# Attention scores of a pair as two 64-row halves of the array, with three products each

## The chip, the cores and the metric

The kernel runs on one core of one Trainium2 chip. Its engines are TensorE (PE in the profile; its weight loads are listed apart, as PEld), VectorE (DVE), ScalarE (ACT), GpSimd (POOL) and SyncE (SP), whose queue issues most of the transfers. The metric is the device time of one execution in microseconds.

## The reference, cut to what matters

Two layers of an encoder for 512 positions and width 1024. Each layer normalizes, projects with one matrix of 4096 columns, runs two groups of attention, gates both, and projects back. All is in float32.

```python
# per layer; q_a, k_a, v_a: 8 heads of 64; q_b, k_b: 4 heads of two maps of 64; v_b: 4 heads of 128
proj = rmsnorm(x, norm_g[l]) @ w_in[l]
# group A: every position sees an 8 x 16 window of the 8 x 64 grid
logits = einsum('bhcd,bhicjd->bhcij', qr, kr) * 64**-0.5 + bias
out_a  = softmax(logits) @ v                      # per head
# group B: two softmax maps over all 512 positions, subtracted
logits = einsum('bqhtd,bkhtd->bhtqk', qblk, k) * 64**-0.5   # t = 0, 1
p      = softmax(logits + t5_bias)
out_b  = rmsnorm((p[:, :, 0] - lam * p[:, :, 1]) @ v, subln_g) * (1 - lam_init)
x = x + concat([out_a * silu(g_a), out_b * silu(g_b)]) @ w_out[l]
```

## The kernel before, in words

Every float32 factor is held as a sum of a high and a low part in a shorter format (fp32r), and a product is computed as three: high by high, high by low, low by high. For the projections (`proj_fm`, L252, with 512 columns; `proj_tm`, L267, with 256) these are 24 matrix products per PSUM tile, 8 slices of the contraction in three terms.

A layer goes through the list `ORDER`: V units (VB, VA), Q units (QB, QA: 128 columns of q and 128 of k, so two heads of group A or the two maps of one head of group B), attention steps (AB, AA) and gates. One Q unit gives the pair that one attention step works on.

*Evacuation.* `evac_q` (L271) takes the PSUM tile of q, whose rows 0 to 63 belong to the first of the pair and 64 to 127 to the second, and makes two tiles of it, one per map or head: in each, rows 0 to 63 hold the high part (ScalarE, L276) and rows 64 to 127 the low part (VectorE, L277). `evac_k` (L282) writes the high and low parts of both k into rows 0 to 63 (L290, L291), and a transfer on SP's queue (L292) copies these rows to rows 64 to 127. So a score product contracts over 128 rows, (q high, q low) by (k high, k high), and a second one over (q high, q low) by (k low, k low): two products per map.

*Group B* (`attn_b`, L303). For each of 4 tiles of 128 queries and each of 2 maps: two products of 512 columns into `st` (L316, L317), an addition of the bias with a running minimum (L319, VectorE, a custom instruction), the exponential (L322, ScalarE). Then the weights of both maps are scaled and subtracted (L326 to L329), transposed on PE (L333), split (`split`, L205 and L206) and multiplied with v into `pv` (L338).

*Group A* (`attn_a`, L363), called once per head: the bias tile `ba` is built on GpSimd (L179). For each of 4 query tiles: two products of 256 columns into `st` (L370), addition with minimum (L376), exponential (L379), scaling (L381, L382), two transposes (L385), split; at the end eight products with v (L392).

*PSUM.* Eight banks: `ps_p` has three tiles (`pp`, projections), `ps_s` two of one bank (`st`, scores, also the first warm-up products, L462, the transposed gain, L468, and the bias table, L151), `ps_t` two (`pt`), `ps_v` one (`pv`).

*Order.* Up to the first unit the order is pinned as written (`pinned`, `held`). Behind that a planner (the Tile framework with its timeline) decides the order on each engine: it fills PE with projection products between the steps of attention. Weights come through two raw buffers (`wraw`, SP's queue, L84), are cast on ScalarE (L99), and their low part is computed on GpSimd (L101).

Of the kernel before, what the change touches and what calls it, by code (L numbers as in the profile page):

```python
# [9 lines left out]
F32 = mybir.dt.float32  # L10
F32R = mybir.dt.float32r
AF = mybir.ActivationFunctionType
# [4 lines left out]
P = 128  # L17
S = 512
# [26 lines left out]
def hybrid_encoder(ctx: ExitStack, tc: tile.TileContext, x, norm_g, w_in, na_rpb,  # L45
# [14 lines left out]
    ps_s = ctx.enter_context(tc.tile_pool(name="ps_s", bufs=2, space=PSUM))  # L60
# [15 lines left out]
    # ---------------------------------------------------------------- weights  # L76
# [47 lines left out]
    # ------------------------------------------------------- position biases  # L124
# [60 lines left out]
    # ------------------------------------------------------------- lambdas  # L185
# [22 lines left out]
    # ---------------------------------------------------------------- norm  # L208
# [35 lines left out]
    # --------------------------------------------------------- projections  # L244
# [26 lines left out]
    def evac_q(pp):  # L271
        res = []
        for m in range(2):
            q = qk.tile([P, S], F32R, name="qs", bufs=QK_BUFS)
            src = pp[64 * m:64 * m + 64, :]
            A.activation(out=q[0:64], in_=src, func=AF.Copy, scale=-0.125)  # L276
            V.scalar_tensor_tensor(out=q[64:128], in0=src, scalar=-0.125, in1=q[0:64].bitcast(F32),  # L277
                                   op0=ALU.mult, op1=ALU.subtract)
            res.append(q)
        return res  # L280

    def evac_k(pp, natural):  # L282
        kt = qk.tile([P, 4, S], F32R, name="kt", bufs=2)
        for m in range(2):
            src = pp[64 * m:64 * m + 64, :]
            kh, kl = kt[0:64, m, :], kt[0:64, 2 + m, :]
            if natural:
                src = src.rearrange("p (b r c) -> p b r c", r=ROWS, c=C8)
                kh, kl = (z.rearrange("p (r b c) -> p b r c", r=ROWS, c=C8) for z in (kh, kl))
            A.copy(out=kh, in_=src)  # L290
            V.tensor_tensor(out=kl, in0=src, in1=kh.bitcast(F32), op=ALU.subtract)  # L291
        nc.sync.dma_start(out=kt[64:128].bitcast(F32), in_=kt[0:64].bitcast(F32))  # L292
        return [(kt[:, m, :], kt[:, 2 + m, :]) for m in range(2)]
# [368 lines left out]
```

## Time and profile before

| | us |
|---|---|
| median of 3 runs | 632.57 |
| lowest and highest | 631.94, 633.4 |
| span of the profiled execution | 630.6 |
| PE busy | 591.7 |
| VectorE busy | 422.3 |
| ScalarE busy | 324.6 |
| GpSimd busy | 277.3 |

The profile gives no time of its own for the profiled execution beyond the span, which runs from the first to the last instruction. Busy time of PE is modelled at the ends of products, and neighbouring products overlap in it: a product of 512 columns lasts about 0.39 us from start to end, but the next one starts 0.23 us after it. Where it matters, starts are compared with starts.

### The profile page before, as it was taken

How to read it: one execution, taken by the hardware profiler on the slowest of the kernel's cores; microseconds unless marked ns; L12 is line 12 of the kernel's file. 1: busy time of each engine (PE TensorE's matmuls, PEld its weight loads, DVE VectorE, ACT ScalarE, POOL GpSimd, SP SyncE). 2: the span in 40 equal slices, each digit the busy share in tenths (PEclk: the TensorE clock that was granted, in tenths of full speed). 3: DMA queues.
4: the chain of work that ended last, by engine and by line, in shares of the span. 5: the costliest groups of instructions: out<-in, count | busy, mean ns of one | idle time of the engine just before them, and what ended most of it. 6: DMA issues, size and time to landing. Idle time of an engine off the chain costs nothing.

```text
span 630.6 us, 10037 instructions
## 1 busy us (share of the span) xinstructions
PE 591.7 (94%) x3626; PEld 522.3 (83%) x3626; DVE 422.3 (67%) x907; ACT 324.6 (51%) x706; POOL 277.3 (44%) x232
## 2 busy tenths in 40 slices
PE   4799699999899999999999999999989999999992
PEld 3678597888799878889999898888879878889992
DVE  3552354997988868874564257798888968874542
ACT  3343353864766555744343455666567646654421
POOL 2341422444456747743143633344535665733111
PEclk9799899999999999999999999999999999999997
DMA  6566746552442454264454452342343444355204
GB/s 145 129 124 192 213 147 197 134 136 78 109 119 55 143 129 133 85 171 146 134 168 135 123 144 86 90 114 63 88 107 93 116 116 116 101 167 168 68 1 134
DMA packets 77448, 77.57 MB, mean 123 GB/s; under 512 B 9906, under 2 KB 71346, under 8 KB 76374
## 3 DMA queue, kind: packets, MB, share of 16 engines
q1 hardware_dynamic: 75926, 74.53, 41.7%
q0 software_dynamic: 1472, 2.40, 2.3%
q8 instruction: 29, 0.48, 0.3%
q14 instruction: 21, 0.17, 0.1%
HBM read 63.16 MB, written 9.37 MB: 115 GB/s over the span
## 4 chain that ended last, share of the span: by engine, by line
PE 58%; DMA 14%; DVE 10%; issue 5%; POOL 5%; SPq 5%; ACT 3%; POOLq 0%; ACTq 0%; DVEq 0%
PE pp L252 25%; PE pp L267 22%; DMA wraw<-in_w_in_dram 4%; DMA y<-in_x_dram 4%; SPq L135 3%; DVE ea L382 2%; POOL wl L101 2%; DMA yb_d<-tb_d 2%; POOL ba L179 2%; PE pv L338 2%; DVE kt L291 2%; DVE w4k L329 1%; PE pt L333 1%; PE st L316 1%; DMA rs_d<-rsb 1%
## 5 line engine op out<-in xcount | busy, mean ns | idle before, releaser
L101 POOL TENSOR_TENSOR wl<-wraw,wh 128x1024 fp32r<-128x1024 f32 x68 | 166.2, 2462 | 192.5 <-ACT wh L99 124.9
L99 ACT CAST wh<-wraw 128x1024 fp32r<-128x1024 f32 x78 | 78.8, 1046 | 72.2 <-DMA wraw<-in_w_in_dram 28.9
L252 PE MATMUL pp<-hTh,wh 128*128 128x512 f32 x384 | 103.4, 397 | 3.2 <-DVE kt L291 3.2
L252 PE MATMUL pp<-hTh,wl 128*128 128x512 f32 x384 | 106.3, 398 | 0.0
L252 PE MATMUL pp<-hTl,wh 128*128 128x512 f32 x384 | 104.5, 398 | 0.0
L252 PEld LDWEIGHTS pp<-hTh,wh 128*128 128x128 f32 x384 | 70.4, 188 | 17.7 <-issue 3.6
L252 PEld LDWEIGHTS pp<-hTh,wl 128*128 128x128 f32 x384 | 70.3, 189 | 14.5 <-issue 0.5
L252 PEld LDWEIGHTS pp<-hTl,wh 128*128 128x128 f32 x384 | 70.2, 188 | 13.9
L267 PE MATMUL pp<-wh,hTh 128*128 128x256 f32 x256 | 72.3, 302 | 7.7 <-ACT hTh L205 4.5
L267 PE MATMUL pp<-wh,yTh 128*128 128x256 f32 x256 | 72.4, 283 | 0.0
L267 PE MATMUL pp<-wl,yTh 128*128 128x256 f32 x256 | 72.3, 283 | 0.0
L267 PE MATMUL pp<-wh,yTl 128*128 128x256 f32 x256 | 71.9, 283 | 0.0
L267 PE MATMUL pp<-wh,hTl 128*128 128x256 f32 x256 | 70.3, 293 | 0.0
L206 DVE TENSOR_TENSOR ptl<-pt,pth 128x256 fp32r<-128x256 f32 (+1 forms) x96 | 48.2, 507 | 31.6 <-ACT pth L205 30.7
L267 PE MATMUL pp<-wl,hTh 128*128 128x256 f32 x256 | 68.9, 287 | 0.0
L205 ACT CAST pth<-pt 128x256 fp32r<-128x256 f32 (+1 forms) x96 | 42.0, 443 | 43.1 <-PE pt L333 29.3
L382 DVE TENSOR_SCALAR ea<-ea,rza 128x256 f32<-128x256 f32 x64 | 58.5, 914 | 1.8
L267 PEld LDWEIGHTS pp<-wh,hTh 128*128 128x128 f32 x256 | 49.3, 202 | 10.9 <-ACT hTh L205 5.0
L179 POOL TENSOR_TENSOR ba<-nmask,ya 128x256 f32<-128x256 f32 (+1 forms) x64 | 39.6, 650 | 32.3 <-DVE mna L376 18.5
L319 DVE CUSTOM_DVE_ANT_0 lt<-st,yb 128x512 f32<-128x512 f32 x64 | 43.5, 685 | 11.2 <-PE st L317 10.7
L267 PEld LDWEIGHTS pp<-wh,hTl 128*128 128x128 f32 x256 | 48.8, 199 | 0.8
L267 PEld LDWEIGHTS pp<-wh,yTh 128*128 128x128 f32 x256 | 49.1, 192 | 0.2
(111 smaller groups left out, 1141.0 us busy)
## 6 DMA issues: line engine op xcount, KB each, us to landing
wraw<-in_w_in_dram SPq DMA_DIRECT2D x32, 512.0 KB
wraw<-in_w_in_dram SPq DMA_DIRECT2D x64, 256.0 KB
kt<-kt SPq DMA_DIRECT2D x16, 512.0 KB
wraw<-in_w_out_dram SPq DMA_DIRECT2D x16, 512.0 KB
y<-in_x_dram SPq DMA_DIRECT2D x16, 256.0 KB
ya_d<-rp_d SPq DMA_DIRECT2D x32, 120.0 KB
ya<-ya_d SPq DMA_DIRECT2D x16, 240.0 KB
yb<-yb_d SPq DMA_DIRECT2D x8, 280.0 KB
```

The source lines that it names most:

```text
L99: A.copy(out=wh[:, ks, :], in_=r)
L101: eng.tensor_tensor(out=wl[:, ks, :], in0=r, in1=wh[:, ks, :].bitcast(F32), op=ALU.subtract)
L135: eng.dma_start(out=dst[:, i * C8:(i + 1) * C8, :], in_=bass.AP(tensor=src.tensor, offset=src.offset + base - step * r - C8 * b, ap=[[pitc ...
L179: G.tensor_tensor(out=ba[:, i0:i0 + n], in0=_view(nmask, i0 * C8, [[C8, n], [0, ROWS], [1, C8]]), in1=_view(y, w0, [[C8, n], [RPW, ROWS], ...
L205: A.copy(out=oh, in_=ps)
L206: V.tensor_tensor(out=ol, in0=ps, in1=oh.bitcast(F32), op=ALU.subtract)
L252: T.matmul(out=pp, lhsT=a[:, kc, cs], rhs=b[:, kc, c0:c0 + S], start=(n == 0), stop=(n == 3 * KC - 1))
L267: T.matmul(out=pp[:, 0:256], lhsT=a[kc][:, c0:c0 + P], rhs=b[:, kc, :], start=(n == 0), stop=(n == 3 * KC - 1))
L291: V.tensor_tensor(out=kl, in0=src, in1=kh.bitcast(F32), op=ALU.subtract)
L319: V.tensor_tensor_reduce(out=lt, in0=st, in1=yb[:, 48 - 16 * qt:560 - 16 * qt], scale=1.0, scalar=3e38, op0=ALU.add, op1=ALU.min, accum_ou ...
L338: T.matmul(out=pv[:, qp * 256:(qp + 1) * 256], lhsT=vt[:, kt, h % 2, vs, :], rhs=pp[:, kt, :], start=(n == 0), stop=(n == 11))
L382: V.tensor_scalar_mul(e, e, rz)
```

## The change

The pair is computed together. `evac_q` and `evac_k` no longer rearrange rows: they evacuate all 128 rows at once, the high part with one ScalarE instruction and the low part with one VectorE instruction, and the copy of k on SP's queue is gone. A new function `scores` computes the scores of both maps or heads of the pair for one query tile into one `st` tile of two banks: the first map from rows 0 to 63, the second from rows 64 to 127. Each contracts over 64 rows, so three products are needed per map: q high by k high, q low by k high, q high by k low. The two maps alternate. `attn_a` now handles two heads, with two bias tiles at once. `ps_s` has one buffer of two banks where it had two of one, and warm-up, gain and table products use `ps_p`. `qs` keeps two buffers, which held the two maps of one unit and now hold two whole units; `kt` has two buffers of half the size; `ba` has four instead of two. The instructions behind the scores stay the same in number.

```diff
-    ps_s = ctx.enter_context(tc.tile_pool(name="ps_s", bufs=2, space=PSUM))
+    ps_s = ctx.enter_context(tc.tile_pool(name="ps_s", bufs=1, space=PSUM))
...
-            tp = ps_s.tile([P, S], F32, name="st")
+            tp = ps_p.tile([P, S], F32, name="pp")
...
-        ba = work.tile([P, 12, ROWS, C8], F32, name="ba")
+        ba = work.tile([P, 12, ROWS, C8], F32, name="ba", bufs=4)
...
     def evac_q(pp):
-        res = []
-        for m in range(2):
-            q = qk.tile([P, S], F32R, name="qs", bufs=QK_BUFS)
-            src = pp[64 * m:64 * m + 64, :]
-            A.activation(out=q[0:64], in_=src, func=AF.Copy, scale=-0.125)
-            V.scalar_tensor_tensor(out=q[64:128], in0=src, scalar=-0.125, in1=q[0:64].bitcast(F32),
-                                   op0=ALU.mult, op1=ALU.subtract)
-            res.append(q)
-        return res
+        q = qk.tile([P, 2, S], F32R, name="qs", bufs=QK_BUFS)
+        A.activation(out=q[:, 0, :], in_=pp, func=AF.Copy, scale=-0.125)
+        V.scalar_tensor_tensor(out=q[:, 1, :], in0=pp, scalar=-0.125, in1=q[:, 0, :].bitcast(F32),
+                               op0=ALU.mult, op1=ALU.subtract)
+        return q
...
-        nc.sync.dma_start(out=kt[64:128].bitcast(F32), in_=kt[0:64].bitcast(F32))
-        return [(kt[:, m, :], kt[:, 2 + m, :]) for m in range(2)]
+        A.copy(out=kh, in_=src)
+        V.tensor_tensor(out=kl, in0=src, in1=kh.bitcast(F32), op=ALU.subtract)
+        return kt
+
+    def scores(q, qs, keys):
+        st = ps_s.tile([P, 2, S], F32, name="st")
+        for n, (a, b) in enumerate(((0, 0), (1, 0), (0, 1))):
+            for m in range(2):
+                rhs = keys(b, slice(64 * m, 64 * m + 64))
+                out = st[:, m, :] if rhs.shape[-1] == S else st[:, m, 0:256]
+                T.matmul(out=out, lhsT=q[64 * m:64 * m + 64, a, qs], rhs=rhs, start=(n == 0), stop=(n == 2))
+        return st
...
+                st = scores(q, slice(qt * P, (qt + 1) * P), lambda i, ps: k[ps, i, :])
                 for m in range(2):
-                    st = ps_s.tile([P, S], F32, name="st")
-                    kh, kl = k[m]
-                    T.matmul(out=st, lhsT=q[m][:, qt * P:(qt + 1) * P], rhs=kh, start=True, stop=False)
-                    T.matmul(out=st, lhsT=q[m][:, qt * P:(qt + 1) * P], rhs=kl, start=False, stop=True)
```

The planner arranges the new program anew. The first place is PE at the first scores of the first layer, where the second projection of the pair ends and a V unit begins (L316 and L317 before, L294 after are score products; L252 and L267 are projections). Before:

```order
L252 MATMUL pp<-hTh,wl 128x512 x8
L267 MATMUL pp<-wh,hTh 128x256
L267 MATMUL pp<-wl,hTh 128x256
L316 MATMUL st<-kt,qs 128x512
L317 MATMUL st<-kt,qs 128x512
L316 MATMUL st<-kt,qs 128x512
L317 MATMUL st<-kt,qs 128x512
L267 MATMUL pp<-wh,hTl 128x256
```

And after:

```order
L252 MATMUL pp<-hTh,wl 128x512 x6
L294 MATMUL st<-kt,qs 128x512 x6
L252 MATMUL pp<-hTh,wl 128x512 x2
L252 MATMUL pp<-hTh,wh 128x512 x8
L252 MATMUL pp<-hTl,wh 128x512 x8
L252 MATMUL pp<-hTh,wl 128x512 x8
L294 MATMUL st<-kt,qs 128x512 x6
L267 MATMUL pp<-wh,hTh 128x256
```

The first group of scores moves ahead of the next unit's projection, and a whole projection stands between it and the second group.

The second place is PE in group A of the first layer (L370 before and L294 after are score products; L385 and L382 transposes; L390 products with v). Before:

```order
L370 MATMUL st<-kt,qs 128x256 x2
L252 MATMUL pp<-hTh,wh 128x512 x4
L252 MATMUL pp<-hTl,wh 128x512 x8
L252 MATMUL pp<-hTh,wl 128x512 x4
L370 MATMUL st<-kt,qs 128x256 x2
L252 MATMUL pp<-hTh,wl 128x512
L385 MATMUL pt<-ident,ea 128x128 x2
```

And after:

```order
L390 MATMUL pv<-pth,v 128x256
L390 MATMUL pv<-ptl,v 128x256
L294 MATMUL st<-kt,qs 128x256 x5
L382 MATMUL pt<-ident,ea 128x128 x2
L294 MATMUL st<-kt,qs 128x256
L382 MATMUL pt<-ident,ea 128x128 x2
```

Groups of two products each become groups of six, some of which are cut by transposes or products with v; over the program L294 stands in 88 stretches, 36 with 512 columns and 52 with 256, for 64 groups.

## Rows read from the trace of the kernel before

**Rows 1.** Page, part 1: busy us (share of the span) and instructions.
```profile
span 630.6 us, 10037 instructions
...
PE 591.7 (94%) x3626; PEld 522.3 (83%) x3626; DVE 422.3 (67%) x907; ACT 324.6 (51%) x706; POOL 277.3 (44%) x232
```

**Rows 2.** Busy us by stage (length; PE, PEld, DVE, ACT, POOL; PE clock; DMA).
```profile
39.00:175.00 136.00, 125.81 (x694) 107.23 (x693) 88.28 (x195) 69.59 (x140) 50.15 (x38) 0.97 0.55 150
175.00:283.00 108.00, 107.28 (x619) 92.49 (x617) 85.70 (x205) 64.85 (x153) 68.83 (x62) 1.00 0.44 118
283.00:573.00 290.00, 286.68 (x1794) 255.09 (x1793) 205.77 (x444) 157.26 (x344) 132.22 (x96) 1.00 0.41 117
sum 534.00, PE 519.77 PEld 454.81 DVE 379.75 ACT 291.70 POOL 251.20; mean PE 173.26 PEld 151.60 DVE 126.58 ACT 97.23 POOL 83.73
```

**Rows 3.** Chain of waits in order of time: start us, us, what.
```profile
283.40 44.42 PE pp L267 x369
327.82 0.87 PE pt L234 x8
...
347.39 18.82 PE pp L252 x81
...
366.33 0.24 PE st L316
```

**Rows 4.** Groups by line: xcount | busy us, mean ns of one | idle before, releasers.
```profile
L319 DVE CUSTOM_DVE_ANT_0 lt<-st,yb 128x512 f32<-128x512 f32 x64 | 43.5, 685 | 11.2 <-PE st L317 10.7
...
L316 PE MATMUL st<-kt,qs 128*128 128x512 f32 x64 | 26.6, 416 | 2.7 <-DMA kt<-kt 1.6 <-DVE mn L319 1.0
...
L370 PE MATMUL st<-kt,qs 128*128 128x256 f32 x128 | 25.9, 289 | 2.2 <-DMA kt<-kt 1.6 <-DVE mna L376 0.6
...
L277 DVE SCALAR_TENSOR_TENSOR qs<-pp,qs 64x512 fp32r<-64x512 f32 x32 | 22.1, 689 | 4.7 <-ACT qs L276 3.9
L291 DVE TENSOR_TENSOR kt<-pp,kt 64x512 fp32r<-64x512 f32 x32 | 21.9, 686 | 27.9 <-ACT kt L290 27.5
```

**Rows 5.** Weight loads where the table product L151 begins: start us, us, what.
```profile
32.17 0.14 PEld L234 LDWEIGHTS pt<-ident,w4k 128*128 128x128 f32 x1
32.48 0.09 PEld L151 LDWEIGHTS st<-oh,t5s 32*4 32x4 f32 x2 [0.17 <-issue]
```

**Rows 6.** Loads and products where L151 ends, from several overlapping windows.
```profile
34.28 0.19 PEld L267 LDWEIGHTS pp<-wh,hTh 128*128 128x128 f32 x1 [0.86 <-ACT wh L99]
33.34 1.02 PE L151 MATMUL st<-oh,t5s 32*4 32x512 f32 x2
34.28 0.39 PE L267 MATMUL pp<-wh,hTh 128*128 128x256 f32 x1
...
33.77 0.59 PE L151 MATMUL st<-oh,t5s 32*4 32x512 f32 x1
...
34.51 0.64 PE L267 MATMUL pp<-wh,hTh 128*128 128x256 f32 x4
```

**Rows 7.** ScalarE and VectorE in the same stretch.
```profile
31.92 1.25 ACT L205 CAST hTh<-pt 128x512 fp32r<-128x512 f32 x2 [3.54 <-PE pt L234]
...
35.36 0.42 DVE L206 TENSOR_TENSOR v<-pp,v 128x256 fp32r<-128x256 f32 x1 [1.46 <-ACT v L205]
```

**Rows 8.** Products around one with two stationary columns, L349.
```profile
121.40 0.40 PE L252 MATMUL pp<-hTh,wl 128*128 128x512 f32 x1
121.63 0.39 PE L349 MATMUL pv<-sr,ones_r 128*2 128x512 f32 x1
121.86 0.40 PE L252 MATMUL pp<-hTh,wl 128*128 128x512 f32 x1
```

**Rows 9.** Who waited for whom, PE alone: us in total, times, longest us.
```profile
PE pp L267 <- DVE kt L291: 3.2, 1, 3.2
PE pp L252 <- DVE kt L291: 3.2, 2, 1.6
```

**Rows 10.** Chain of waits near 70 us: a weight load.
```profile
67.96 4.69 DMA wraw<-in_w_in_dram
```

More of the change, by code (lines that the diff above doesn't have):

```diff
@@ L367, in attn_a @@
         for j, (k0, dk) in enumerate(A_TILES):
-            st = ps_s.tile([P, S], F32, name="st")
-            for i in range(2):
-                T.matmul(out=st[:, 0:256], lhsT=q[:, j * P:(j + 1) * P],
-                         rhs=k[i].rearrange("p (t c) -> p t c", c=P)[:, k0:k0 + dk + 1:dk, :],
-                         start=(i == 0), stop=(i == 1))
-            e = work.tile([P, 256], F32, name="ea", bufs=3)
-            mn = small.tile([P, 1], F32, name="mna")
-            i0 = (0, 4, 4, 8)[j]
@@ L383, in attn_a @@
-            pt = ps_t.tile([P, 4, P], F32, name="pt")
-            for i in range(2):
-                T.transpose(out=pt[:, i, :], in_=e[:, i * P:(i + 1) * P], identity=ident)
-            t0, sl, stp = A_SLOT[j]
-            oh, ol = (_view(p, t0 * 256 + sl * P, [[stp, 2], [1, P]]) for p in ptt)
-            split(pt[:, 0:2, :], oh, ol)
-        pv = ps_v.tile([P, S], F32, name="pv")
-        for n, (t, q0, dq) in enumerate(A_PV):
-            for i, pp in enumerate(ptt):
-                T.matmul(out=_view(pv, q0, [[dq, 2], [1, P]]), lhsT=vt[:, t, hd % 4, :],
-                         rhs=pp[:, t, :].rearrange("p (a b) -> p a b", b=P),
-                         start=(n == 0 and i == 0), stop=(n == 3 and i == 1))
@@ new lines, in attn_a @@
+            for m in range(2):
+                e = work.tile([P, 256], F32, name="ea", bufs=3)
+                mn = small.tile([P, 1], F32, name="mna")
+                i0 = (0, 4, 4, 8)[j]
+                V.tensor_tensor_reduce(out=e, in0=st[:, m, 0:256],
+                                       in1=ba[m][:, i0:i0 + 4].rearrange("p a b c -> p (a b c)"),
+                                       scale=1.0, scalar=3e38, op0=ALU.add, op1=ALU.min, accum_out=mn)
+                A.activation(out=e, in_=e, func=AF.Exp, bias=mn, scale=-1.0, accum_out=z[:, m, j:j + 1])
+                rz = small.tile([P, 1], F32, name="rza")
+                V.reciprocal(out=rz, in_=z[:, m, j:j + 1])
+                V.tensor_scalar_mul(e, e, rz)
+                pt = ps_t.tile([P, 4, P], F32, name="pt")
+                for i in range(2):
+                    T.transpose(out=pt[:, i, :], in_=e[:, i * P:(i + 1) * P], identity=ident)
+                t0, sl, stp = A_SLOT[j]
+                oh, ol = (_view(t, t0 * 256 + sl * P, [[stp, 2], [1, P]]) for t in ptt[m])
+                split(pt[:, 0:2, :], oh, ol)
@@ new lines, in attn_a @@
+        for m in range(2):
+            pv = ps_v.tile([P, S], F32, name="pv")
+            for n, (t, q0, dq) in enumerate(A_PV):
+                for i, pp in enumerate(ptt[m]):
+                    T.matmul(out=_view(pv, q0, [[dq, 2], [1, P]]), lhsT=vt[:, t, (2 * p + m) % 4, :],
+                             rhs=pp[:, t, :].rearrange("p (a b) -> p a b", b=P),
+                             start=(n == 0 and i == 0), stop=(n == 3 and i == 1))
+            tmp = work.tile([P, S], F32, name="tmpa", tag="s2", bufs=3)
+            lo = 64 * m
+            hi = 64 - lo
+            A.activation(out=tmp[lo:lo + 64], in_=pv[hi:hi + 64], func=AF.Copy, scale=0.5)
+            V.scalar_tensor_tensor(out=s_out[lo:lo + 64], in0=pv[lo:lo + 64], scalar=0.5, in1=tmp[lo:lo + 64],
+                                   op0=ALU.mult, op1=ALU.add)
@@ L459, in warm @@
     def warm(n):
-        wm = ps_s.tile([P, S], F32, name="st")
+        wm = ps_p.tile([P, S], F32, name="pp")
         for i in range(n):
@@ L465, in hybrid_encoder @@
     for i in range(2):
-        gp = ps_s.tile([P, S], F32, name="st")
+        gp = ps_p.tile([P, S], F32, name="pp")
         for j in range(4):
@@ L541, in att_a @@
             q, k = qk_t.pop(0)
[L542 to L544 removed]
+            attn_a(l, p, q, k, v.rearrange("p t h s d -> p t h (s d)"), ys[p])
         qk_t = []
```

42 lines of the change are left out of this document (12 added, 30 removed).

## The prediction, made before the changed kernel ran

> **What bounds the kernel now.** I read the busy table first, then the stages, then the chain of waits, then single matrix products. TensorE (PE) is busy 591.7 of 630.6 us, VectorE 422.3, ScalarE 324.6 [rows 1]. By stages, PE is busy 125.81 of 136 us in group B of the first layer, 107.28 of 108 in group A, and 286.68 of 290 from there to the last projection; from 39 to 573 us it is idle for 534.0 - 519.8 = 14.2 us [rows 2]. VectorE is the next one, with 85.70 of 108 us at its fullest. PE's busy time can hide gaps, because neighbouring products overlap in the trace, so I also checked the spacing on the chain of waits: 81 products of 512 columns in 18.82 us are 0.232 us each, 369 of 256 columns in 44.42 us are 0.120 us each, and a score product takes 0.24 us [rows 3]. These are long runs without a hole. So the end is set by the sum of what PE has to stream, plus some 14 us of waits, and every microsecond that a change adds to PE's own queue between 39 and 573 us shows nearly whole in the time. What it saves on VectorE, ScalarE and the DMA queues shows only where PE now waits for them.
>
> **Slots removed.** Scores now are 64 products of 512 columns at L316 and as many at L317, and 128 of 256 at L370 [rows 4]: 128 x 0.232 + 128 x 0.120 = 45.1 us of PE.
>
> **Slots added.** The new helper issues 6 products per pair instead of 4: 192 of 512 columns and 192 of 256, each with 64 rows, alternating between the upper and the lower half of the array. No product of the trace runs beside another one, so I bound this from both sides. If the two halves stream at the same time, three pairs take three slots: 96 x 0.232 + 96 x 0.120 = 33.8 us, a change of -11.3. If a half waits for the other, it is 67.6 us, a change of +22.5. Between them lies a case for which there is a near row. Each product brings its own weight load, and eight transposes, which stream little and are held up by their loads, take 0.87 us [rows 3]: one load of 128 columns every 0.109 us. If loads still follow one another and only streams overlap, a group of six has its last product start 5 x 0.109 = 0.545 us after the first, and takes 0.545 + 0.232 = 0.777 us with 512 columns (before: 0.928) and 0.665 with 256 (before: 0.480). Over 32 groups each that is 24.9 + 21.3 = 46.2 us, a change of +1.1: what group B wins, group A loses, since its short streams do not cover two loads. I take this value, since every pair of loads in the trace keeps this distance.
>
> **Changing between the two shapes.** PE enters the half-row shape and leaves it again for each stretch of score products. The order of the new program has 88 stretches of L294, not 64, because the planner cuts 24 of the groups with transposes or value products; so 176 changes. The trace has one place where the array's row split changes: the table product L151 with 32 rows amid products with 128. Going in, the last load of a transpose is at 32.17 and the next would follow 0.109 later, at 32.28; it comes at 32.48, 0.20 late, with nothing to wait for ("issue") [rows 5]. Coming out, the last two L151 products are 0.43 apart, so the slot after 33.77 ends at 34.20; the next load starts at 34.28, and its product, with the load no longer hidden behind a stream, holds the array until 34.51, that is 0.23 instead of 0.12: together 0.08 + 0.11 = 0.19 [rows 6]. The row names the cast of L99, whose output this product does not read; it reads hTh, cast by 31.92 + 1.25 = 33.17 [rows 7], so I take the delay as PE's own. At 0.19 us each, 176 changes are 33.4 us. This is the largest term, and it rests on one place with a 32-row shape; the bounds are 0 (the chip treats a half like the whole) and 0.20 (35.2 us).
>
> A counter-row stands beside it: the product with a 2-column stationary operand, L349, starts 0.23 us after its neighbour (121.40 to 121.63) and is followed after another 0.23 [rows 8]. So narrowing the columns costs nothing, and splitting the rows does. The Trainium skill, TensorEngine Tiling (Array Packing), section Key Properties, says that changing the tiling mode, and not merely the tile, drains the engine. By that rule both places should have stalled; the trace agrees for the 32-row one (0.19 to 0.20 us) and not for the 2-column one. Taken for rows alone the rule gives the 33.4 us, taken by L349's row 0.
>
> **Evacuation and copies.** Each of 16 projection units loses two of its four VectorE subtractions (0.689 and 0.686 us [rows 4]), 22.0 us in all, since 128 partitions are done at once, and two of its four ScalarE casts. Both engines are covered by PE, so in itself this is worth nothing; were PE not there, it would be worth up to those 22 us. The 16 copies of k leave SP's queue, so the weight loads behind them no longer wait for the subtractions that each copy needs, and q has room for two units instead of one. What PE can gain is its waits: 1.6 + 1.6 us for the copy [rows 4] and 3.2 + 3.2 us for L291, which releases a projection's PSUM tile [rows 9], 9.6 in all, and at the utmost all of its 14.2 us of idleness. Half of the second goes with half of the subtractions; behind the copy stands the subtraction, which stays, so of the first I count half too: -4.8, bounds 0 and -14.2.
>
> **The added wait.** ps_s had two buffers of one bank; now it has one tile of two. The next six products wait until both reductions of the previous tile are read; before, the first two waited for the first reduction only. Queued behind the waiting product on PE is everything else: projections, transposes and value products, and with them the weights' buffers. PE waits 1.0 + 0.6 us for reductions now; one reduction more is 0.685 us [rows 4]. The planner puts projection work between groups, as the order shows, so I take twice the present wait, +1.6, bounds 0 and +5. At the start, warm-up and table products move to the projections' ring of three, and the third projection of the first unit must wait for the second's value cast, which VectorE ends at 35.36 + 0.42 = 35.78, instead of starting at 34.28 [rows 6, 7]: 1.5 us. Further on PE waits behind a weight load that lands at 67.96 + 4.69 = 72.65 [rows 10], whatever PE did before, so I count 0, bound +1.5.
>
> **The sum.** -45.1 + 46.2 + 33.4 - 4.8 + 1.6 = +31.3. The profiled span is 630.6 us and the median of the runs 632.57, so 2.0 lies around the span; I leave that as it is. 630.6 + 31.3 + 2.0 = **663.9**. With the other ends of the small terms (-14.2 to 0 for the relief, 0 to 6.5 for the waits, 0.18 to 0.20 per change) the same case gives 651 to 675.
>
> **Rivals.**
> (a) The halves load and stream wholly side by side, and changes cost as in the trace: -11.3 instead of +1.1, so 651.5. For it: the halves use other rows and other banks. Against: no two loads in the trace overlap. The Trainium skill, TensorE: Matmul & The Clock Gate, section Part 3, tells of four 32-row tiles of 512 columns that ran 3.07 times as fast as in turn. By that figure, an estimate, a product of a pair takes 0.77 of a perfect overlap's rate and the scores 33.8 / 0.77 = 44 us, 2 us off my middle; no run here shows it.
> (b) The halves run in turn: 663.9 - 1.1 + 22.5 = 685.3. For it: products in the trace start strictly in turn.
> (c) **Faster**: the change of shape between 64 and 128 rows costs nothing, as with L349. Then 663.9 - 33.4 = 630.5 with loads in turn and 618.1 with loads side by side. Its place is the 176 borders, and it decides from a price per border: with side-by-side loads the kernel gets faster below (11.3 + 3.2) / 176 = 0.08 us, with loads in turn below 0.01. Against it: 0.19 in the only row that splits rows.
> (d) The diff does not do what it says: borders are free but halves run in turn: 630.5 - 1.1 + 22.5 = 651.9, the 6-for-4 products then being a plain addition.
>
> **How the numbers follow.** Forecast (borders cost, streams overlap, loads in turn) 0.45; (a) 0.17; (b) 0.10; (c) 0.20; (d) 0.08. The range leaves (c) out and takes in the others: 640 (case (a) with the whole relief) to 688 (case (b) with its waits). About 0.2%, 1.3 us, is what a measurement of this kernel tells from no change. Faster by more: nearly all of (c), 0.19; within: its upper end, 0.03; slower: 0.78.
>
> **What would show it.** In the trace after: at each border of L294 a load that starts some 0.1 to 0.2 us after the previous slot is over and a first product held for another 0.1; if loads follow the previous start at once, the forecast falls and (c) holds. Inside a group: six starts some 0.11 apart (forecast), in pairs of equal start (a), or 0.23 apart with 512 columns (b, d). L294's loads and products should be followed by the same VectorE rows, with fewer and no longer casts of qs and kt, and PE's waits for the copy gone. Wrong on the small side would be a wait for the reductions beyond 5 us, or weights arriving so much earlier that PE's 10 us of idleness in the first B stage vanish.

## The result and the profile after

| | before | after |
|---|---|---|
| median of the runs, us | 632.99 (631.94 to 633.88) | 650.67 (650.1 to 651.44) |
| after / before | | 1.0284 (95%: 1.0266 to 1.0302) |
| span of the profiled execution, us | 630.6 | 648.3 |

The change makes the kernel slower by 17.7 us, in the medians and in the spans alike. Of the texts ahead, the forecast of 663.9 has the sign and the borders as the cause. Two rivals have the time: (a), halves side by side and borders that cost, with 651.5, and (d), halves in turn and borders free, with 651.9. The starts below decide for (a).

The page of the kernel after, part 1 (busy us, share of the span, instructions), answers to [rows 1]:

```profile
span 648.3 us, 10112 instructions
...
PE 613.4 (95%) x3754; PEld 516.0 (80%) x3754; DVE 387.3 (60%) x875; ACT 303.8 (47%) x674; POOL 279.5 (43%) x232
```

VectorE got 35.0 us lighter and ScalarE 20.8, and it did not help: PE got 21.7 us heavier. The stages of the kernel after, in the columns of [rows 2] (length; PE, PEld, DVE, ACT, POOL; PE clock; DMA):

```profile
39.00:175.00 136.00, 130.28 (x751) 105.33 (x751) 87.51 (x199) 66.16 (x138) 56.95 (x49) 0.97 0.47 134
175.00:283.00 108.00, 107.42 (x592) 86.34 (x592) 68.02 (x177) 54.23 (x134) 63.32 (x55) 1.00 0.33 95
283.00:573.00 290.00, 288.23 (x1814) 243.81 (x1813) 178.37 (x415) 142.45 (x318) 125.39 (x90) 1.00 0.33 97
```

Over the three stages (the same stretches of time, in which the slower kernel gets less far) PE is idle for 534.0 - 525.9 = 8.1 us, where it was 14.2. The granted clock of each stage is what it was. So PE waits less, and yet the end comes later: the loss is inside what the profile calls busy, and only the starts of products show it. One border pair of group B, from the timeline of the kernel after (start us, us, engine, line, operation, tile; from several overlapping windows, first the products, then the weight loads):

```profile
57.58 0.40 PE L252 MATMUL pp<-hTh,wl 128*128 128x512 f32 x1
57.91 0.50 PE L294 MATMUL st<-kt,qs 64*128 64x512 f32 x2
...
58.47 0.40 PE L294 MATMUL st<-kt,qs 64*128 64x512 f32 x2
58.80 0.50 PE L252 MATMUL pp<-hTh,wl 128*128 128x512 f32 x1
...
57.91 0.19 PEld L294 LDWEIGHTS st<-kt,qs 64*128 64x128 f32 x2 [0.37 <-issue]
...
58.25 0.19 PEld L294 LDWEIGHTS st<-kt,qs 64*128 64x128 f32 x2
...
58.80 0.19 PEld L252 LDWEIGHTS pp<-hTh,wl 128*128 128x128 f32 x1 [0.37 <-issue]
58.91 0.19 PEld L252 LDWEIGHTS pp<-hTh,wl 128*128 128x128 f32 x1
59.14 0.19 PEld L252 LDWEIGHTS pp<-hTh,wh 128*128 128x128 f32 x1
```

Three things are to be seen. First, "x2": two products, one of each half, and two loads, one of each half, start within the same 0.01 us; in the raw starts of all 178 such pairs the loads are mostly 3 to 4 ns apart, and the products at most 10 ns. Second, from 57.58 to 57.91 and from 58.47 to 58.80 there is 0.33 us where a product of 512 columns needs 0.23: the array is run empty before the row split changes, and the weight load behind the border waits with it ("issue": it waited for nothing that the profile shows). Third, the product behind each border lasts 0.50 instead of 0.40: its load could not hide behind the product ahead of it. The raw starts of this group, each product's (ns from the start of the L252 at 57.58), give the sizes:

```
L252 0 | L294 327, 330 | 661, 665 | 889, 893 | L252 1217
slots:       0.232 + 0.095  0.334     0.228     0.232 + 0.096 us
```

Over all stretches the middle delay is 0.093 us at an entry and 0.088 at an exit; and the first pair of a stretch comes 0.334 us ahead of the second, where inner pairs keep 0.228: 0.105 for the load that is not hidden (0.055 where the product behind the border is a transpose of 128 columns, at 10 of the exits). So a border costs 0.09 + 0.105 = 0.195 us.

With these prices I divided the time of PE, from 39 us to its last product, from start to start: a slot of 0.232, 0.120 or 0.109 us for 512, 256 or 128 columns (once for a pair that starts together), 0.195 for each border, and the rest. The rest holds waits, stretches at a lower granted clock, and whatever the fixed prices miss. The few ns between the two starts of a pair are in no column; they add up to 0.65 us in the kernel after and to at most 1.2 in the others. This table is my own sum and no view of the profile; each of the kernels under it is told of below.

| kernel | median us | slots, 128 rows | slots, 64 rows | borders | rest |
|---|---|---|---|---|---|
| before | 632.99 | 559.2 | 0 | 0 | 21.0 |
| after | 650.67 | 514.1 | 35.7 | 34.3 (176) | 12.5 |
| e1: two tiles of one bank | 678.76 | 514.5 | 58.0 | 47.6 (244) | 6.3 |
| e2: one map behind the other | 656.16 | 514.5 | 43.5 | 37.4 (192) | 3.8 |
| e3: longer stretches in A | 642.25 | 515.0 | 35.2 | 27.3 (140) | 11.5 |
| e4: more borders | 666.70 | 518.0 | 35.0 | 57.7 (296) | 2.8 |
| t1: stretches uncut | 641.62 | 514.5 | 33.8 | 25.0 (128) | 14.4 |
| t2: uncut and longer | 636.49 | 514.8 | 33.8 | 18.7 (96) | 18.5 |
| t3: four banks a stretch | 748.12 | 518.2 | 33.8 | 9.4 (48) | 130.8 |
| t4: evacuation in two pieces | 662.45 | 515.3 | 36.7 | 38.2 (196) | 19.2 |
| e5: halves in group B alone | 681.37 | 527.5 | 22.3 | 14.8 (76) | 60.9 |

From before to after: -45.1 + 35.7 + 34.3 - 8.5 = +16.4 us, of 17.7 in the spans.

Groups of the kernel after (xcount | busy us, mean ns | idle before, releasers), answering to [rows 4]:

```profile
L294 PE MATMUL st<-kt,qs 64*128 64x512 f32 (+1 forms) x384 | 59.6, 384 | 5.2 <-DVE mn L318 5.2
L294 PEld LDWEIGHTS st<-kt,qs 64*128 64x128 f32 x384 | 32.1, 186 | 26.5 <-issue 11.9 <-DVE mn L318 5.7 <-DVE w4k L327 1.5
...
L274 DVE SCALAR_TENSOR_TENSOR qs<-pp,qs 128x512 fp32r<-128x512 f32 x16 | 11.0, 686 | 3.0 <-ACT qs L273 3.0
L285 DVE TENSOR_TENSOR kt<-pp,kt 128x512 fp32r<-128x512 f32 x16 | 11.0, 686 | 22.6 <-ACT kt L284 22.6
```

A subtraction of 128 partitions takes 0.686 us, as one of 64 did, so 22 us are gone from VectorE as reckoned. The copy of k and the waits for L291 have no row any more (9.6 us before, [rows 4, 9]). The waits for reductions are longer, 5.2 us against 1.6, but 4.2 of that are one place, which the kernel before has too under other names. PE's wait in the kernel after (us in total, times, longest), answering to [rows 9]:

```profile
PE st L294 <- DVE mn L318: 5.2, 2, 4.2
```

The chain of waits of the kernel after shows the place (start us, us, what):

```profile
66.03 4.79 DMA wraw<-in_w_in_dram
...
70.89 1.04 ACT wh L99
71.94 0.49 ACT kt L284
...
72.46 0.69 DVE kt L285
73.15 0.60 DVE lt L318
...
73.75 0.60 DVE lt L318
...
74.42 1.65 PE st L294 x6
76.07 4.76 PE pp L267 x21
```

The two reductions stand in VectorE's queue behind the evacuation of k, and PE's next six products wait for both, with the projection L267 behind them in PE's queue. But the evacuation of k is late because its cast (L284) stands on ScalarE behind the cast of a weight tile (L99), whose transfer lands at 70.82. In the kernel before, the load of [rows 10] lands at 72.65 and the same chain follows it:

```profile
72.72 1.04 ACT wh L99
73.79 0.59 ACT kt L290
...
74.40 0.70 DVE kt L291
```

There PE waits 0.98 us for a reduction (L316 at 70.67, [rows 4]) and 3.23 for this L291 (L267 at 75.24, [rows 9]), together 4.2 as well. So this place is the same in both kernels. What is really gone are the copy's 3.2 us and the other 3.2 for L291, and the waits for reductions elsewhere went from 0.6 to 1.0. In e1, e3, e4, t1 and t2 the longest wait for a reduction, 3.2 to 4.6 us, is at this place too.

### The profile page after: what moved, and what is told of

The parts are those of the page before. It is cut to its first block, busy times and chain, and to the rows that moved or that the text cites. A ratio compares the mean times of both kernels' runs of the same rounds, so it can differ in the third digit from the quotient of the medians.

```text
span 648.3 us, 10112 instructions
## 1 busy us (share of the span) xinstructions
PE 613.4 (95%) x3754; PEld 516.0 (80%) x3754; DVE 387.3 (60%) x875; ACT 303.8 (47%) x674; POOL 279.5 (43%) x232
## 4 chain that ended last, share of the span: by engine, by line
PE 77%; DVE 7%; DMA 6%; ACT 5%; SPq 2%; issue 2%; POOL 0%; POOLq 0%; ACTq 0%
PE pp L252 34%; PE pp L267 26%; PE st L294 7%; DMA y<-in_x_dram 3%; PE pv L337 3%; PE pt L382 2%; PE pv L390 2%; PE pt L332 2%; SPq L135 2%; ACT wh L99 2%; DVE ea L379 2%; DVE yTl L206 2%; DMA yb_d<-tb_d 1%; PE pt L234 1%; DMA wraw<-in_w_in_dram 1%
## 5 line engine op out<-in xcount | busy, mean ns | idle before, releaser
L101 POOL TENSOR_TENSOR wl<-wraw,wh 128x1024 fp32r<-128x1024 f32 x68 | 168.0, 2486 | 169.6 <-ACT wh L99 123.2
L99 ACT CAST wh<-wraw 128x1024 fp32r<-128x1024 f32 x78 | 78.5, 1047 | 62.4 <-issue 20.5
L252 PE MATMUL pp<-hTl,wh 128*128 128x512 f32 x384 | 104.8, 401 | 0.0
L252 PE MATMUL pp<-hTh,wl 128*128 128x512 f32 x384 | 102.6, 400 | 0.0
L252 PE MATMUL pp<-hTh,wh 128*128 128x512 f32 x384 | 102.1, 398 | 0.0
L252 PEld LDWEIGHTS pp<-hTl,wh 128*128 128x128 f32 x384 | 70.6, 188 | 18.2 <-issue 2.5
L252 PEld LDWEIGHTS pp<-hTh,wl 128*128 128x128 f32 x384 | 70.7, 189 | 17.0 <-issue 2.2
L252 PEld LDWEIGHTS pp<-hTh,wh 128*128 128x128 f32 x384 | 70.1, 188 | 16.8 <-issue 2.2
L267 PE MATMUL pp<-wh,hTh 128*128 128x256 f32 x256 | 72.1, 301 | 5.0 <-ACT hTh L205 4.7
L267 PE MATMUL pp<-wh,yTh 128*128 128x256 f32 x256 | 72.6, 284 | 2.4 <-ACT yTh L205 1.8
L267 PE MATMUL pp<-wl,yTh 128*128 128x256 f32 x256 | 72.2, 283 | 0.0
L267 PE MATMUL pp<-wh,yTl 128*128 128x256 f32 x256 | 71.5, 283 | 0.0
L267 PE MATMUL pp<-wh,hTl 128*128 128x256 f32 x256 | 71.3, 297 | 0.0
L267 PE MATMUL pp<-wl,hTh 128*128 128x256 f32 x256 | 70.3, 292 | 0.0
L294 PE MATMUL st<-kt,qs 64*128 64x512 f32 (+1 forms) x384 | 59.6, 384 | 5.2 <-DVE mn L318 5.2
L205 ACT CAST pth<-pt 128x256 fp32r<-128x256 f32 (+1 forms) x96 | 40.2, 443 | 45.3 <-PE pt L332 28.7
L267 PEld LDWEIGHTS pp<-wh,hTh 128*128 128x128 f32 x256 | 49.0, 201 | 8.8 <-ACT hTh L205 5.2
L321 ACT ACTIVATE w4k<-lt,mn 128x512 f32<-128x512 f32 x64 | 45.8, 718 | 21.7 <-DVE mn L318 21.6
L294 PEld LDWEIGHTS st<-kt,qs 64*128 64x128 f32 x384 | 32.1, 186 | 26.5 <-issue 11.9
L267 PEld LDWEIGHTS pp<-wh,yTh 128*128 128x128 f32 x256 | 49.1, 192 | 3.3 <-ACT yTh L205 2.2
```

Source lines behind the costliest of these rows:

```text
L99: A.copy(out=wh[:, ks, :], in_=r)
L101: eng.tensor_tensor(out=wl[:, ks, :], in0=r, in1=wh[:, ks, :].bitcast(F32), op=ALU.subtract)
L205: A.copy(out=oh, in_=ps)
L252: T.matmul(out=pp, lhsT=a[:, kc, cs], rhs=b[:, kc, c0:c0 + S], start=(n == 0), stop=(n == 3 * KC - 1))
L267: T.matmul(out=pp[:, 0:256], lhsT=a[kc][:, c0:c0 + P], rhs=b[:, kc, :], start=(n == 0), stop=(n == 3 * KC - 1))
L294: T.matmul(out=out, lhsT=q[64 * m:64 * m + 64, a, qs], rhs=rhs, start=(n == 0), stop=(n == 2))
```

## The experiments

### What the two halves do, and what the tile of two banks is for

**e1_two_tiles**: as the kernel after, but two tiles of one bank.

```diff
-    ps_s = ctx.enter_context(tc.tile_pool(name="ps_s", bufs=1, space=PSUM))
+    ps_s = ctx.enter_context(tc.tile_pool(name="ps_s", bufs=2, space=PSUM))
...
-        st = ps_s.tile([P, 2, S], F32, name="st")
+        st = [ps_s.tile([P, S], F32, name="st") for _ in range(2)]
```

> The changed kernel with the scores in two tiles of one bank (ring of two) instead of one tile of two banks, so that a bank is free as soon as its own reduction has read it. The planner then makes 122 stretches of score products instead of 88. If the single tile's wait matters (PE waits 5.2 us for the reductions in the profile after), up to 5 us are won: 645 us. If borders are what counts, 34 x 2 x 0.197 = +13.4 us: 664 us, less what the earlier release gives back: 659 to 664 us.

Measured: 678.76 us, 1.0722 of before (1.0678 to 1.0765). Neither expectation had that. The wait for two reductions at once did shrink, but with a tile of its own each map came free at another time, and the planner issued the three products of one map as soon as its bank was free: 52 pairs were left of 192, and 280 products ran alone, in 122 stretches. The same 384 products keep PE busy half as long again (group of e1):

```profile
L294 PE MATMUL st<-kt,qs 64*128 64x512 f32 (+1 forms) x384 | 90.7, 375 | 3.2 <-DVE mn L318 3.2
```

In the table: slots of half rows +22.3 us, borders +13.3, rest -6.2. So 126 broken pairs cost 22.3 / 126 = 0.18 us each, between the slots of 256 and of 512 columns (0.120 and 0.232), which is what a product costs that has nobody beside it. The tile of two banks is what holds the maps together; its longer wait (5.2 us against 3.2) is the price, and cheap beside the 28 us that e1 lost.

**e2_in_turn**: the three products of one map, then those of the other.

```diff
-        for n, (a, b) in enumerate(((0, 0), (1, 0), (0, 1))):
-            for m in range(2):
+        for m in range(2):
+            for n, (a, b) in enumerate(((0, 0), (1, 0), (0, 1))):
```

> The changed kernel with the loops of scores exchanged: the three products of the first map come first, then the three of the second, so that five slots in a row are needed where the alternating order needs three if halves stream side by side. The order of the program has 96 stretches of score products instead of 88. If the halves overlap fully in the changed kernel (rival a of the prediction): 32 x 2 x (0.232 + 0.120) = +22.5 us for the slots and 8 x 2 x 0.197 = +3.2 for the borders, so 676 us. If the alternating order brought no overlap, the slots stay as they are: 650.7 + 3.2 = 654.

Measured: 656.16 us, 1.0367 of before (1.0314 to 1.0421). This edit did not do what it says: the planner alternated most of the products again, and 128 pairs ran side by side, with 128 products alone, in 96 stretches. So it settles less than it was made for: that the time lies near the 654 us expected for no overlap is no evidence for it. What can be read: 50 pairs fewer than after (178) and +7.8 us of slots, 0.16 us for each broken pair, as in e1.

### What a border costs

**e4_more_borders**: into each group behind its first two products a product of 128 rows and 32 columns with zeros, so the group is cut by it. It adds nothing to the scores.

```diff
+            if n == 0:
+                T.matmul(out=st[:, 0, 0:32], lhsT=zero_r, rhs=zero_r[:, 0:32], start=False, stop=False)
```

> The changed kernel with one more product per group behind the first pair: 128 rows of zeros, 32 columns, added into the scores (it adds zero). Each takes the array out of the half-row shape and back, 128 more borders, and the order has 94 stretches instead of 88. If borders cost 0.197 us each: (128 + 12) x 0.197 = +27.6 us and some 64 x 0.03 for the products' own streams, so 680 us. If borders cost nothing and a product costs its load: 64 x 0.109 = +7.0, so 658 us.

Measured: 666.7 us, 1.0548 of before (1.0504 to 1.0591), 16.0 us over after, between the two expectations. The groups of e4:

```profile
L296 PE MATMUL st<-kt,qs 64*128 64x512 f32 (+1 forms) x384 | 75.0, 415 | 4.6 <-DVE mn L322 4.6
...
L298 PE MATMUL st<-zero_r 128*128 128x32 f32 x64 | 17.9, 279 | 0.0
```

The products of the scores are the same, yet they last 415 ns instead of 384: more of them are first in their stretch and show their own load. In the table the 120 additional borders are +23.4 us and the slots of the zero products +3.9; the rest falls by 9.7. The price per border holds in the starts: at 52 places where a zero product stands between two pairs, the second pair comes 0.41 us later than its slot, two borders (0.39) and 0.02 for the product itself, for which the table's 0.06 is too much. So some 2.4 us of the fall of the rest are the table's; another part are waits that are over by the time PE comes to them: those for `yTh`, `ea`, `y` and `ptl`, 3.6 us in the kernel after, have no row in e4. By the time alone a border of e4 costs only (16.0 - 1.5) / 120 = 0.12 us, with 1.5 us for the zero products.

**e3_longer**: two query tiles of group A per stretch, in one tile of two banks.

```diff
-        for j, (k0, dk) in enumerate(A_TILES):
-            st = scores(q, slice(j * P, (j + 1) * P),
...
+        for jp in (0, 2):
+            st = ps_s.tile([P, 2, S], F32, name="st")
+            for jj in range(2):
...
+                        T.matmul(out=st[:, m, 256 * jj:256 * jj + 256], lhsT=q[ps, a, (jp + jj) * P:(jp + jj + 1) * P],
```

> The changed kernel, but group A puts the scores of two query tiles into one pair of banks (12 products in a row into the two halves of each bank), with 70 stretches in the order instead of 88, all else and all products the same. If the loss is the price of a border (0.197 us each, drain and exposed load): 36 borders fewer, -7.1 us, 643.6 us. If the loss came from the third product per map or from the loss of a score buffer, nothing is gained, and the longer hold of the banks costs: 650.7 or more.

Measured: 642.25 us, 1.0147 of before (1.0081 to 1.0214); 8.4 us under after, where the price of borders had said 643.6. There are 70 stretches instead of 88, so 36 borders fewer: 0.23 us each in the time, 0.195 in the starts.

**t1_uncut**: the planner may not cut a group.

```diff
-        for n, (a, b) in enumerate(((0, 0), (1, 0), (0, 1))):
+        with tc.high_priority():
+          for n, (a, b) in enumerate(((0, 0), (1, 0), (0, 1))):
```

> The changed kernel with the six products of a group given priority over other work in the planner, so that no group is cut: 64 stretches instead of 88, the same products. If each border costs 0.195 us as in the trace: 48 borders fewer, -9.4 us, and all products paired again, -1.9: 639.4 us, at most 645 if PE's waits grow where other work is pushed back. If the cuts lay where PE had to wait anyway, nothing changes: 650 us.

Measured: 641.62 us, 1.0171 of before (1.0137 to 1.0205). All 192 pairs start together, in 64 stretches. 48 borders fewer, 9.05 us less: 0.19 each, or 0.15 if t1 and after are each set against the runs of the kernel before beside them (1.0171 and 1.0284). Its group, beside 59.6 in after:

```profile
L295 PE MATMUL st<-kt,qs 64*128 64x512 f32 (+1 forms) x384 | 51.7, 375 | 5.0 <-DVE mn L319 5.0
```

**t2_uncut_long**: t1 and e3 together.

> As the last, and group A with the scores of two query tiles (12 products) in one stretch: 48 stretches instead of 88. Borders: -80 x 0.195 = -15.6 us, pairs -1.9: 633 us, level with the kernel before, if PE's waits stay at 12.5 us; up to 640 if the longer hold of the banks makes PE wait. If borders are not what counts: 650 us.

Measured: 636.49 us, 1.0082 of before (1.0056 to 1.0108): 80 borders fewer than after, 14.2 us less, 0.18 each (0.16 by the ratios). It is the best form of the change that I found, and still 0.8% slower than before. Its groups:

```profile
L295 PE MATMUL st<-kt,qs 64*128 64x512 f32 x192 | 31.6, 434 | 7.3 <-DVE mn L319 7.3
...
L375 PE MATMUL st<-kt,qs 64*128 64x256 f32 x192 | 15.6, 295 | 0.0
```

The products of group B wait 7.3 us for reductions, against 5.0 in t1; the place at the weight load is much the same (4.2 and 4.6), and why another wait of 3.1 comes at 134.7 us was not tested. By the table, slots are 559.2 - 514.8 - 33.8 = 10.6 us less than before, the borders take 18.7 and the rest gives 2.5 back: +5.6, and +6.4 with the 0.8 us between the starts of its pairs, of 6.6 in the spans (637.2 against 630.6).

**t3_four_banks**: one tile of four banks, two query tiles of group B or all four of group A per stretch. The banks come from the projections (two instead of three) and the transposes (one instead of two).

```diff
-    ps_p = ctx.enter_context(tc.tile_pool(name="ps_p", bufs=3, space=PSUM))
+    ps_p = ctx.enter_context(tc.tile_pool(name="ps_p", bufs=2, space=PSUM))
...
-    ps_t = ctx.enter_context(tc.tile_pool(name="ps_t", bufs=2, space=PSUM))
+    ps_t = ctx.enter_context(tc.tile_pool(name="ps_t", bufs=1, space=PSUM))
...
+                st4 = ps_s.tile([P, 2, 2, S], F32, name="st")
```

> Four banks for the scores (projections two instead of three, transposes one instead of two): group B takes two query tiles in one stretch, group A all four, 24 stretches. Borders: -128 x 0.195 = -25.0 us, pairs -1.9: 623.8 us, faster than the kernel before, if PE's waits stay at 12.5 us. The rival: with fewer banks elsewhere and all scores' banks released only after the last reduction, PE waits longer; with 15 us more it is 639 us, with 30 us more 654.

Measured: 748.12 us, 1.1861 of before (1.1821 to 1.1902). Far off both expectations. The borders are as planned, 24 stretches and 9.4 us, and the rest is 130.8. PE's waits in t3 (us in total, times, longest):

```profile
PE pt L393 <- DVE ptl L206: 14.4, 16, 1.7
PE pt L234 <- DVE hTl L206: 10.4, 6, 4.2
PE pp L267 <- ACT yTh L205: 10.3, 6, 3.4
PE pp L267 <- DVE v L206: 9.4, 4, 2.4
```

Transposes wait for the only `pt` to be split, and projections for a `pp` to be evacuated. Such waits are not the whole of the rest: from 39 to 732 us PE is idle for 693.0 - 613.9 = 79.1 us, and the mean granted clock in that stretch is 0.91, where it is 0.99 in the kernels before and after from 39 us to their last product, so more products ran at the lower of its two levels. The stretch of t3, in the columns of [rows 2]:

```profile
39.00:732.00 693.00, 613.85 (x3645) 524.89 (x3646) 369.71 (x854) 293.06 (x648) 267.32 (x211) 0.91 0.31 90
```

The longer stretches are to be had only for banks that others need more.

### Where the relief came from

**t4_pieces**: as after, but q and k evacuated in two pieces of 64 rows each, as many instructions as before and no copy.

```diff
-        A.activation(out=q[:, 0, :], in_=pp, func=AF.Copy, scale=-0.125)
-        V.scalar_tensor_tensor(out=q[:, 1, :], in0=pp, scalar=-0.125, in1=q[:, 0, :].bitcast(F32),
-                               op0=ALU.mult, op1=ALU.subtract)
+        for m in range(2):
+            ps = slice(64 * m, 64 * m + 64)
+            A.activation(out=q[ps, 0, :], in_=pp[ps, :], func=AF.Copy, scale=-0.125)
+            V.scalar_tensor_tensor(out=q[ps, 1, :], in0=pp[ps, :], scalar=-0.125, in1=q[ps, 0, :].bitcast(F32),
+                                   op0=ALU.mult, op1=ALU.subtract)
```

> The changed kernel with each evacuation of q and k in two pieces of 64 rows, as many ScalarE and VectorE instructions as in the kernel before (32 more casts and 32 more subtractions), no copy of k; the order has 98 stretches instead of 88. If the evacuations are covered by PE, as the prediction has it: +20 x 0.195 = +3.9 us for the borders alone, 654.6 us. If they hold PE up, as the doubled evacuation of k did: 660 to 680 us.

Measured: 662.45 us, 1.0478 of before (1.0443 to 1.0513), 11.8 us over after. The planner, too, cuts ten more stretches: borders +3.9, slots +2.2. The rest is +6.7: by this reading, evacuations that VectorE and ScalarE have plenty of time for still hold PE up. The new order of the planner came with them, and no run tells the two apart. The page and a wait of t4:

```profile
PE 620.2 (94%) x3754; PEld 520.8 (79%) x3754; DVE 405.0 (61%) x907; ACT 325.1 (49%) x706; POOL 275.9 (42%) x232
...
PE pp L267 <- ACT yTh L205: 6.8, 2, 3.4
```

VectorE is at 61%, so a share of busy time does not tell that its instructions are without price. This wait was 1.8 us in after.

**e8_k_engines** and **e7_q_room**: the kernel before, with one part of the change each. In e8 the copy of k goes, and the engines write both halves of `kt`; in e7 q has one buffer more; **e9_both** has both.

```diff
+            for lo in (0, 64):
+                kh, kl = kt[lo:lo + 64, m, :], kt[lo:lo + 64, 2 + m, :]
...
-        nc.sync.dma_start(out=kt[64:128].bitcast(F32), in_=kt[0:64].bitcast(F32))
...
-            q = qk.tile([P, S], F32R, name="qs", bufs=QK_BUFS)
+            q = qk.tile([P, S], F32R, name="qs", bufs=QK_BUFS + 1)
```

> The kernel before with three buffers for q instead of two (a buffer holds one map), nothing else: what of the shrunken waits of the changed kernel comes from the room for q. If the room matters, PE's waits (21 us in the kernel before from 39 us on, counted by starts) fall by up to 4 us: 629 us. If not: 632.5.

> The kernel before without the 16 copies of k on SP's queue: ScalarE and VectorE write the high and low parts of k into both halves of the rows themselves, with 32 more casts and 32 more subtractions (18.5 and 21.9 us more of engines that PE covers). If the copy's wait and its place in SP's queue matter: PE's waits fall by 3 to 6 us, 627 to 630 us. If the doubled evacuation holds up the projections' banks instead: 634 to 638 us.

> The kernel before with both: k written into both row halves by the engines, no copy, and three buffers for q. If the two effects add: 625 to 629 us, the fastest of the study. If VectorE's added 22 us in stages where it is busy 80% hold PE up: 632 us or more.

Measured: e7 635.23 us (1.0046, 1.0019 to 1.0074), e8 662.14 (1.0472, 1.0431 to 1.0514), e9 648.55 (1.0259, 1.0217 to 1.03). e7 and e8 missed both of their expectations; e9 is on the side of its second. Room for q alone gives nothing, and is 0.5% slower; in e8, with its added evacuation, it takes back nearly half of the loss. By the same sum as in the table the rest is 22.4, 51.5 and 35.0 us, with no borders. In e8 the waits for the copy are gone and the time is 4.7% longer: 32 more subtractions and as many casts, in a new order, stand ahead of what PE waits for. Page and groups of e8:

```profile
PE 607.7 (92%) x3626; PEld 533.9 (81%) x3626; DVE 437.8 (66%) x939; ACT 344.1 (52%) x738; POOL 278.4 (42%) x232
...
L317 PE MATMUL st<-kt,qs 128*128 128x512 f32 x64 | 26.8, 419 | 9.2 <-DVE mn L320 7.3 <-DVE qs L277 1.3 <-ACT kt L292 0.6
```

In e8 the score products wait 7.3 us for the reduction of the tile before, 1.0 in [rows 4]; 5.6 of this is one wait that ends at 77.59, again behind the cast of a weight tile (L99 at 73.05), where PE waited 4.2 in the kernel before. Other waits are spread over many places. Two stretches of e8, columns as in [rows 2]:

```profile
110.00:122.00 12.00, 8.95 (x36) 5.99 (x35) 11.36 (x17) 8.23 (x18) 5.70 (x4) 0.87 0.44 132
122.00:125.00 3.00, 3.00 (x8) 2.32 (x8) 2.94 (x8) 1.21 (x3) 0.56 (x1) 0.50 0.05 3
```

PE is idle for 3 of 12 us while VectorE is busy for 11.4, and the mean granted clock of this stretch is 0.87; in the next it is 0.50, the lower of the two levels (1.2 GHz), and 8 products take 3 us. Over the whole span e8 has a mean granted clock of 0.955, before and after 0.981 each. How much of e8's loss is the clock and how much the waits was not taken apart.

### Whether one of the groups loses more

**e5_b_only**: halves in group B; group A with its old evacuation, products and copy of k, its `st` tiles two by two in the tile of two banks.

```diff
+            eq, ek = (evac_q, evac_k) if nat else (evac_q_old, evac_k_old)
...
+            if j % 2 == 0:
+                st2 = ps_s.tile([P, 2, S], F32, name="st")
+            st = st2[:, j % 2, :]
```

> Only group B computes its scores in 64-row halves, as in the changed kernel; group A takes its scores as before, with two products of 128 rows per head and query tile, with q and k evacuated and k copied as before (q has room for one unit only, the banks of the scores are shared two by two). The order has 38 stretches of half-row products. If the loss goes by the number of borders: 76 x 0.195 = +14.8 us, slots -29.7 + 22.7 = -7.0, so +7.8 before PE's waits shrink; these shrank by 8.5 us in the changed kernel and by perhaps 4 here: 633 to 641 us, likeliest 637. If the loss lies in the evacuation, the score banks or group B's three products, group B alone keeps most of it: 645 or more.

Measured: 681.37 us, 1.0773 of before (1.0729 to 1.0816). Borders came down to 14.8 us as meant, but the rest rose to 60.9. The mixture took away what both kernels have, a bank per map in group A and room for a unit of q. The waits for the reductions of group A, and perhaps those of its transposes, fit the first; for the second no row was found; and at a mean granted clock of 0.955 a part of the rest is the clock. What each of these cost was not taken apart:

```profile
PE pt L411 <- DVE ea L408: 11.0, 10, 3.8
...
PE st L396 <- DVE mna L402: 5.5, 9, 1.0
```

So it says nothing on the groups. What the prices give is an estimate only: group B wins 29.7 - 22.3 = 7.4 us of slots and pays 72 borders, 14.0; group A wins 15.4 - 11.5 = 3.9 and pays 104, 20.3. By this estimate both groups lose, B 6.6 us and A 16.4. The 9.8 us between the two were not measured by a run of their own; e3, which touches A alone and gains 8.4, is the nearest.

## Why the prediction was right, and where its sizes were off

**PE sets the end: held.** 17.7 us longer, while VectorE, ScalarE and SP's queue all got lighter.

**Borders cost 0.19 us, in all 33.4: held.** 34.3 us by the starts. In the time, a border is worth 0.15 to 0.24 us in e3, t1 and t2, by medians or by ratios, and only 0.12 in e4, where the rest fell. The one place with a 32-row shape was a good source, and both its parts came back: the empty array (0.08 there, 0.09 here) and the load that is not hidden (0.11 and 0.105). The counter-row, the product with two stationary columns [rows 8], did not apply, and rival (c) falls with it. The Trainium skill, TensorEngine Tiling (Array Packing), section Key Properties, says that a change of the tiling mode drains the engine, and gives no price; the trace of after agrees for 64 rows against 128, with 0.09 us each way, and shows as much again for the load. The prediction set [rows 8] against this rule as well; but that section does not say that a product with two stationary columns changes the mode, so the row neither bears the rule out nor speaks against it.

**Two halves stream side by side, but loads in turn: half wrong.** This is the step that failed. The forecast put loads 0.109 us apart because every pair of loads in the trace of before was said to keep that distance, and no two to overlap. That reading was wrong for that trace already: most loads are listed as 0.19 us long and start before the one ahead is over, at 15 places loads for transposes start 57 to 64 ns apart, and the first two loads of L151, the only loads into a part of the rows, start 5 ns apart (the "x2" within 0.09 us of [rows 5]). These two have 4 columns, so they give no price, but they were the nearer row, and they spoke for rival (a). In the kernel after, loads into different halves start mostly 3 to 4 ns apart. The term is 35.7 us instead of 46.2: the 33.8 of a perfect overlap, and 1.9 for the 28 products that the planner left without a partner. Rival (a) had this, at a chance of 0.17. That its time is only 0.8 us off is in part luck: its sum had 4.6 us too little relief, and 1.9 for the broken pairs, 0.9 for the borders and 0.6 behind PE's last product were missing in it, which nearly cancels. The Trainium skill, TensorE: Matmul & The Clock Gate, section Part 3, had led to an estimate of 44 us for overlapping tiles that reach 0.77 of the perfect rate; that figure is of four tiles, and the trace does not agree with carrying it over to two halves: their pairs follow one another every 0.23 us (0.228 at the place above, 0.235 in the middle of 28), the full rate of one product of 512 columns.

**Relief, -4.8: too small.** I counted half of the 9.6 us of waits for the copy and for L291. All of these rows are gone, but 3.2 of them were the wait behind the weight load, which stays under another name; so 6.4 went. Half was reasoned from half of the subtractions staying. In t4, with twice as many evacuation instructions and an order of its own, 6.7 us of the rest come back, at other waits, so "Both engines are covered by PE, so in itself this is worth nothing" was probably too strong.

**Added wait for reductions, +1.6: too large.** The waits that name a reduction went from 1.6 to 5.2 us, +3.6, inside the bounds (0 to 5). But at the weight load PE waits 4.2 us in both kernels, and elsewhere the waits for reductions grew by 0.4 only. The two terms together were -3.2 and measured -8.5 in the rest, -7.8 with the 0.65 us between the starts of pairs, or -6.1 in PE's idle time over the three stages (-6.4 + 0.4 = -6.0 by the waits named here); the counts differ because a busy PE is not always a PE that starts products at its rate.

**Start and weights, 0.** Held: both kernels have started 141 products by 39 us, so the start cost nothing. Of the 1.3 us that the sum lacks (17.7 - 16.4), 0.65 are the offsets within pairs, and 0.6 lie behind PE's last product, which starts 11.4 us before the end of the span in before and 12.0 in after. PE's idle time in the first stage of group B, which the prediction named as what could make it wrong on the small side, went from 10.2 to 5.7 us: half of it, not all.

So the sum had +31.3 and the spans say +17.7: 10.5 of the difference is the loads, 4.6 the waits, less 0.9 for the borders and 0.6 behind the last product.

## What to carry to other kernels

Two half-row products side by side are worth it only in long stretches: a group of six products saves one slot of four, 0.232 us with 512 columns or 0.120 with 256, and each stretch costs two borders, 0.39 us, so by these prices two groups of the first kind or four of the second must stand between borders before anything is won. No run here won: the one that got that far, t3, paid for it in banks. Look for what the scheduler does between the products, since it may cut a stretch, break the pairs, or wait with all of it, and a PSUM tile that spans both products is what keeps them together. And where a trace has nearly one kind of a thing only, as loads into the whole array here, it gives no price for another kind: that is a case for wide bounds, and for a second look at the few rows of the other kind. Last, a wait's name is that of the last link: follow the chain to its start in both kernels before one wait is called gone and another new.

## What the runs showed of the hardware that I had not expected

- Loads into the two halves of the array run side by side, mostly 3 to 4 ns apart at the start, and so do the products (at most 10 ns in the kernel after); a pair keeps the rate of one product, 0.23 us for 512 columns.
- A border between 128 and 64 rows costs the same in both directions (0.093 us in, 0.088 out), and the load behind it is another 0.105 us for products of either shape, 0.055 for transposes.
- In e8 PE was idle for 3 us of 12, and in the next 3 us the granted clock was 0.50, though PE was busy throughout.
